# Sums of x made sooner, x copied back one chunk at a time, and one block of x kept at another address

## The chip, the cores and the metric

The kernel runs on one core of one Trainium2 chip. The metric is the device time of one execution in microseconds (us). Inside the core TensorE (PE) multiplies, VectorE (DVE) and ScalarE (ACT) work on tiles, GpSimd (POOL) and SyncE (SP) issue transfers among other things; each has an instruction queue of its own, which it works off in order, and waits on semaphores where it needs another's result.

## The reference

Two layers: a stick-breaking attention, then an RG-LRU block, each followed by a squared-ReLU MLP of width 4096, on 512 positions of width 1024. The change touches the two MLPs alone:

```python
def squared_relu_mlp(h, w1, w2):
    u = jax.nn.relu(h @ w1)
    return (u * u) @ w2
...
        h = rms_norm(x, norm_mlp[layer])
        x = x + squared_relu_mlp(h, mlp_w1[layer], mlp_w2[layer])
```

## The kernel before, in words

All matrices are f32, and each product is made of three f32r products: a number is split in a coarse part and a remainder, and coarse×coarse, coarse×remainder and remainder×coarse are added in PSUM. So every weight tile is first cast on ACT (`wh`) and subtracted on DVE (`wl`), and so is x.

**x.** x, scaled by the norm's gain, stands transposed in one tile `xg`: eight chunks of 128 features by 512 positions for the coarse part (`xgh`) and eight for the remainder (`xgl`), with margins of 64 elements (`FRONT`) at the ends and between the two. `Chunks` turns a chunk and columns into a place in the tile; its `down` holds two shifts in elements: the first for the first 256 columns of chunk 0, the second for all else. While the MLP's first quarter runs, both are 0. Then `x_down` sets them to 64 and 16 (`ASIDE`), and `lower` copies what is still needed of x down in the tile by as much. In the built program the 128-column blocks of the weights stand 512 bytes apart; after the shift by 64 elements the first columns of chunk 0 stand at a whole multiple of 512 bytes from them (this is the "distance 0"), everything else at 320 bytes past one.

**The MLP.** The 4096 hidden features are worked off in four quarters. The first quarter's up-projection (`squared`, eight output chunks c, plain products of 512 columns) is followed by its down-projection, and each later quarter is an "up" and a "down" of seven block products P1 to P7 with additions between blocks in the manner of Strassen (28 steps of a quarter: 14 of up, 14 of down). An up step is 24 matmuls of 256 columns, a down step 12 of 512. The products of up need sums of blocks of x: for each k of 0 to 3, `sums_of_x(k)` scales chunks k and 4+k on ACT and makes four sums of 256 columns on DVE, and `halves_of_sums(k)` splits them (casts on ACT, subtractions into `low` tiles on DVE). Chunk k must be through with `squared` before its sums may overwrite it in `xg`; sums made earlier are parked (`s3`, and the free eighth chunk of `bh` and `bl`), and `replace` copies them into `xg` later.

**What is made when, before.** In layer 0 the sums of k = 0 and 1 are made while the first up-projection's last output chunks c = 4 and 5 run, in layer 1 those of k = 0, 1 and 2 at c = 4, 5, 6. The others come while the first down runs: after its steps 5 and 6 (`place` 19 and 20) for k = 2 in layer 0 and k = 3 in layer 1, and after steps 10 and 11 (`place` 24 and 25) for k = 3 in layer 0. `replace` copies all parked sums at once after step 7 (`place` 21).

**What sets the order.** PE's order is the program's. On DVE and ACT, from the end of the first up-projection on, each instruction is chained to the one before it (`Ordered`), so they run as written; before that a scheduler merges the streams. `prepare` makes the weights of the step four ahead: a cast on ACT (`wh`), a subtraction on DVE (`wl`), and, where a product needs a sum of two weight blocks, an addition on DVE (`b<-b,b`) or, for P7 and P4, a transfer by POOL that adds the second block in memory to the first in place (L1089). In the first half of up the steps come in the order P1 P5 P6 P3 P7 P2 P4; P1, P6, P7 and P4 add up in one PSUM bank, whose state ACT copies out after P1, P6 and P7 (`u<-ps_acc`, in the second half `u<-ps_z`) before PE may go on in it.

Of the kernel before, what the change touches and what calls it, by code (L numbers as in the profile page):

```python
# [18 lines left out]
S = 512  # L19
D = 1024  # L20
C = D // P
# [6 lines left out]
ASIDE, FRONT = 16, 64  # L28
# [34 lines left out]
def hybrid_encoder(  # L63
# [40 lines left out]
    def f(ap):  # L104
        return ap.bitcast(F32)
# [28 lines left out]
    xgh, xgl = Chunks(0), Chunks(1)  # L134

    def x_down(*down):

        xgh.down = xgl.down = down
    bh = const.tile([P, C, S], F32R, tag="bh", name="bh")
    bl = const.tile([P, C, S], F32R, tag="bl", name="bl")  # L140

# [622 lines left out]
    HS = S // 2  # L764
# [21 lines left out]
    class Mlp:  # L786
# [157 lines left out]
        def halves_of_sums(self, k):  # L944
# [14 lines left out]
            self.A.copy(self.s41[:, k, :], v)  # L959
            self.V.tensor_tensor(low, v, f(self.s41[:, k, :]), ALU.subtract)  # L960

        LOWER = {15: (0, 0), 16: (1, 0), 17: (0, 1), 18: (0, 2), 22: (1, 1), 23: (1, 2)}

        def lower(self, i, part):

            def at(a, n):
                return x_t[:, a : a + n]

            def firsts(a):
                return at(a, 3 * S).rearrange("p (c s) -> p c s", s=S)[:, :, :HS]  # L970

            a = (xgh, xgl)[i].start
            if part:
                a += 2 * (part + 1) * S
                self.A.copy(at(a - ASIDE, 2 * S), at(a, 2 * S))
                return
            self.A.copy(at(a - FRONT, HS), at(a, HS))
            self.A.copy(firsts(a + S - ASIDE), firsts(a + S))

        def replace(self):  # L980

            for k in list(self.s3):
                self.A.copy(xgh[:, k, HS:], f(self.s3[k]))
                here = self.s2(k)
                del self.s3[k]
                self.A.copy(self.s2(k), f(here))

        def slots_of(self, p):

# [154 lines left out]
        def run(self, first, between, end):  # L1144
# [13 lines left out]
            def place(i):  # L1158

                return (i + self.STEPS // 2) % self.STEPS  # L1160
# [8 lines left out]
            def add(i, ahead=1):  # L1169

                if i >= len(steps) or i in done or steps[i][3] not in ("P5", "P6"):
                    return
                *what, name = steps[i]
                far = what[0] == "down" and (name, what[2]) in FARS
                if ahead > (5 if far else 2 if name == "P5" else what[0] == "up"):
                    return
                if steps.index((*what, {"P5": "P1", "P6": "P5"}[name])) in made:
                    done.add(i)

                    self.added(unit(i), name, far=far)  # L1180
# [11 lines left out]
            def prepare(i):  # L1192

                if i < len(steps) and steps[i][0] == "up" and steps[i][3] == "P7":
                    return
                if i - 1 in range(len(steps)) and i - 1 not in made and i > 2:
                    make(i - 1)
                if i < len(steps) and steps[i][0] == "down":
                    add(i, 0)
                    if waiting and place(i) in (20, 22, 23):  # L1200
                        self.split_slot(*waiting.pop(0))
                make(i)
                for n in range(i + 1, i + 6):
                    add(n, n - i)

            def last_sums(u, which):
                for to, a, b, how in which:
                    self.V.tensor_tensor(u[to], u[a], u[b], how)
# [23 lines left out]
            def leave(i):  # L1232

                ahead = i + 4
                if i < 0:
                    return
                kind, q4, p, name = steps[i]
                bank = sums[kind, q4, p if kind == "up" else 0][self.PRODUCTS[name][3]]
                if kind == "down":
                    if q4 == 0 and place(i) == 21:  # L1240
                        self.replace()
                    if p:
                        self.collect(name, 0, bank[0])
                    if steps[min(ahead, len(steps) - 1)][0] == "down":
                        add(ahead, 0)
                    if p:
                        self.collect(name, 1, bank[1])
                    prepare(ahead)
                    if later and place(i) > 15:
                        later.pop()()  # L1250
                    if q4 == 0:
                        x_down(FRONT, ASIDE)
                        if place(i) in self.LOWER:
                            self.lower(*self.LOWER[place(i)])

                        k = ({19: 2, 20: 2, 24: 3, 25: 3}, {19: 3, 20: 3})[self.layer].get(place(i))
                        if k:
                            (self.sums_of_x if place(i) in (19, 24) else self.halves_of_sums)(k)
                    return
                u, three = us[p], bank.rearrange("p (i n) -> p i n", i=2)  # L1260
                keep = {"P1": 0, "P6": 1, "P5": 2, "P7": 3}.get(name)
                if keep is not None:

                    self.A.copy(u[keep], three)
                at, x, y, op = {
                    "P3": (1, three, u[1], ALU.subtract),
                    "P7": (2, u[2], u[3], ALU.subtract),
                    "P2": (0, u[0], three, ALU.add),
                    "P4": (3, three, None, None),
                }.get(name, (None,) * 4)  # L1270
                if op:
                    self.V.tensor_tensor(u[at], x, y, op)
                if name == "P4":
                    def fourth(u=u, three=three, p=p):
                        self.A.activation(u[3], three, AF.Relu)
                        self.square(u[3])
                        if p:
                            last_sums(u, self.SUMS[:2])
                        else:
                            self.sums(p, slice(0, 2))  # L1280

                    if p:
                        fourth()
                    else:
                        later.append(fourth)
                elif later:
                    later.pop()()
                prepare(ahead)
                if op:
                    def rest(u=u, at=at):  # L1290
                        self.A.activation(u[at], u[at], AF.Relu)
                        self.square(u[at])
                        if p:
                            self.split_slot(p, u[at], at)

                    if p and name == "P3":
                        later.append(rest)
                    else:
                        rest()
                    if name == "P2" and not p:  # L1300
                        self.split(p, slice(0, 2), slice(0, 3), slice(0, 3))
                elif name == "P4" and p:
                    last_sums(u, self.SUMS[2:3])
                    self.split_slot(p, u[2], 5)
                    later.append(lambda: last_sums(u, self.SUMS[3:]))
                    waiting[:] = [(p, u[j], 3 + j) for j in (0, 1, 3)]
                elif name in ("P5", "P6") and p:
                    n = ("P5", "P6").index(name)
                    self.split(0, n, slice(0, 4), slice(3, 7))
# [36 lines left out]
        def quarters(self, between, end):  # L1346
            for c in range(C - 1):
                self.squared(c)
                p, i = c // 4, c % 4 // 2
                if c % 2:  # L1350
                    self.split(p, i, slice(0, 3), slice(0, 3))
                    self.sums(p, i)
                    self.split(p, i, slice(0, 4), slice(3, 7))
                if c == 0:
                    units = self.from_down(0)
                    self.load(units, *self.FROM_UP)
                if c < 2:

                    for n in range(4 * c, 4 * c + 4):
                        self.sq.chunk(n, x[n], e=V)  # L1360
                if c == C - 2:
                    self.rr = self.sq.inv_squares(self.bank())
                between(c)

                k = c - 4
                if k in range(2 + self.layer):
                    with tc.issue_after(self.squares.ins):
                        self.sums_of_x(k)
                        self.halves_of_sums(k)
            self.run(units, between, end)  # L1370
            self.blocks.close()
# [460 lines left out]
```

## Time and profile before

| | us |
|---|---|
| median of 3 runs | 1035.24 |
| lowest and highest | 1034.46, 1035.85 |
| the profiled execution | 1034.89 |
| its span on the core | 1033.2 |

PE's granted clock was 0.999 over the span. Layer 0's first down begins at 291.03 us and its first up at 329.93 us; layer 1's first down begins at 757.78 us and its first up at 796.80 us. In the rows of a timeline the first number is the start in us, the second the time of the group, then engine, line, operation and tiles; a bracket tells how long the engine had been idle before and on whom it waited. A matmul's own time overlaps with the next one's, so what a matmul costs is the distance from its start to the next start.

### The profile page before, as it was taken

Reading aid. Unit: us, or ns where it says so; the run is one execution under the profiler, and the core shown is the slowest. Engines: PE = TensorE matmul, PEld = TensorE weight load, DVE = VectorE, ACT = ScalarE, POOL = GpSimd, SP = SyncE. Lnnn points to the kernel's source line nnn. Section 1 sums busy time; section 2 is a strip of 40 time slices with the busy share of each in tenths; the row PEclk is TensorE's granted clock in tenths of the full one; section 3 lists DMA queues with packets and bytes.
Section 4 is the critical chain, followed back from the end, with each engine's and each line's share of the span. In section 5 each row is a group of like instructions: output and inputs, shape, how many; then the busy total and the mean of one; then the engine's idle time right before and its main releaser. Section 6 shows DMA issues by size and latency. Waiting matters only on the chain.

```text
span 1033.2 us, 15885 instructions
## 1 busy us (share of the span) xinstructions
PE 1022.3 (99%) x5868; PEld 892.2 (86%) x5868; DVE 862.9 (84%) x1152; ACT 713.5 (69%) x1104; POOL 174.6 (17%) x235
## 2 busy tenths in 40 slices
PE   9999999999999999999999999999999999999997
PEld 7888888888888988988988888888888988988986
DVE  6988787847789699799799889984689899798898
ACT  6777676836778674774765689964777774874866
POOL 0444444420010010010011210300000010010012
PEclk9999999999999999999999999999999999999999
DMA  7745454537546667677683464452436677677663
GB/s 233 220 121 143 107 154 103 153 108 279 143 82 183 167 154 196 164 158 191 162 233 83 132 179 122 119 202 83 102 80 185 164 163 189 165 159 195 165 125 105
DMA packets 52700, 159.41 MB, mean 154 GB/s; under 512 B 6672, under 2 KB 7952, under 8 KB 52624
## 3 DMA queue, kind: packets, MB, share of 16 engines
q1 hardware_dynamic: 41376, 119.35, 35.8%
q0 software_dynamic: 10528, 38.28, 22.3%
q8 instruction: 46, 0.75, 0.3%
q10 hardware_dynamic: 720, 0.79, 0.2%
q14 instruction: 30, 0.25, 0.1%
HBM read 137.41 MB, written 4.19 MB: 137 GB/s over the span
## 4 chain that ended last, share of the span: by engine, by line
PE 89%; DVE 4%; ACT 3%; issue 2%; DMA 1%; POOL 0%; SPq 0%; DVEq 0%; ACTq 0%; POOLq 0%
PE ps_t L1107 13%; PE ps_acc L1012 8%; PE ps_z L1012 7%; PE ps_acc L1107 7%; PE ps_acc L236 5%; PE ps_acc L238 5%; PE ps_acc L237 5%; PE ps_o L1012 4%; PE ps_z L1107 3%; PE ps_t L236 3%; PE ps_t L237 3%; PE ps_t L238 3%; PE ps_o L236 2%; PE ps_o L237 2%; PE ps_o L238 2%
## 5 line engine op out<-in xcount | busy, mean ns | idle before, releaser
L776 ACT CAST wh<-b 128x1024 fp32r<-128x1024 f32 x168 | 174.1, 1050 | 112.5 <-DVE b L776 73.9
L776 DVE TENSOR_TENSOR wl<-b,wh 128x1024 fp32r<-128x1024 f32 x168 | 204.2, 1221 | 45.4 <-ACT wh L776 44.7
L1089 POOL DMA_DIRECT2D b<-in_w_dn x40 | 35.0, 876 | 352.0 <-DVE b L776 265.6
L236 PE MATMUL ps_acc<-xg,wh 128*128 128x512 f32 x200 | 81.6, 408 | 0.0
L1012 PE MATMUL ps_z<-xg,wh 128*128 128x256 f32 x384 | 79.0, 277 | 0.8 <-ACT u L776 0.8
L238 PE MATMUL ps_acc<-xg,wh 128*128 128x512 f32 x200 | 78.3, 392 | 0.0
L237 PE MATMUL ps_acc<-xg,wl 128*128 128x512 f32 x200 | 78.3, 391 | 0.0
L231 DVE TENSOR_TENSOR wl<-raw,wh 128x512 fp32r<-128x512 f32 (+2 forms) x70 | 62.2, 914 | 15.0 <-ACT wh L229 14.8
L600 DVE TENSOR_TENSOR_SCAN scan<-keep,later 128x128 f32<-128x128 f32 (+1 forms) x64 | 59.5, 933 | 16.2 <-ACT keep L590 9.9
L776 ACT ACTIVATE u<-u 128x512 f32<-128x512 f32 x100 | 63.1, 632 | 9.5 <-DVE u L776 7.7
L229 ACT CAST wh<-raw 128x512 fp32r<-128x512 f32 (+2 forms) x70 | 50.6, 758 | 23.9 <-PE ps_acc L238 7.3
L1012 PE MATMUL ps_z<-xg,wl 128*128 128x256 f32 x240 | 66.4, 277 | 0.0
L1012 PEld LDWEIGHTS ps_z<-xg,wh 128*128 128x128 f32 x384 | 62.8, 188 | 1.2 <-ACT u L776 1.0
L1012 PE MATMUL ps_acc<-xg,wh 128*128 128x256 f32 x288 | 61.6, 278 | 1.2 <-ACT u L776 1.2
L1089 POOL DMA_DIRECT2D b<-in_w_up x24 | 20.9, 870 | 241.8 <-DVE b L776 90.5
L604 POOL TENSOR_TENSOR w<-w,scan 128x128 f32<-128x128 f32 (+1 forms) x64 | 51.4, 805 | 54.4 <-DVE scan L600 51.4
L776 DVE TENSOR_TENSOR b<-b,b 128x1024 f32<-128x1024 f32 x48 | 58.7, 1224 | 1.3
L776 DVE TENSOR_TENSOR u<-u 128x512 f32<-128x512 f32 (+1 forms) x92 | 54.9, 597 | 2.6 <-ACT u L776 1.1
L1012 PE MATMUL ps_acc<-low,wh 128*128 128x256 f32 x192 | 53.2, 277 | 0.1
L1012 PE MATMUL ps_acc<-xg,wl 128*128 128x256 f32 x192 | 53.2, 277 | 0.0
L776 ACT CAST wh<-raw 128x1024 fp32r<-128x1024 f32 x46 | 48.0, 1045 | 6.9 <-PE ps_acc L1107 6.9
L1107 PE MATMUL ps_t<-wh,bh 128*128 128x512 f32 x126 | 49.4, 392 | 0.4 <-DVE c L776 0.4
(383 smaller groups left out, 3277.1 us busy)
## 6 DMA issues: line engine op xcount, KB each, us to landing
b<-in_w_dn SPq DMA_DIRECT2D x48, 512.0 KB, 4.6
b<-in_w_dn POOLq DMA_DIRECT2D x40, 512.0 KB, 5.5
b<-in_w_up SPq DMA_DIRECT2D x36, 512.0 KB, 4.6
b<-in_w_up POOLq DMA_DIRECT2D x24, 512.0 KB, 5.5
raw<-in_w_m SPq DMA_DIRECT2D x16, 512.0 KB, 4.3
raw<-in_w_dn SPq DMA_DIRECT2D x16, 512.0 KB, 4.6
raw<-in_w_in SPq DMA_DIRECT2D x16, 512.0 KB, 4.6
raw<-in_w_qk SPq DMA_DIRECT2D x12, 512.0 KB, 3.7
```

The source lines that it names most:

```text
L229: A.copy(wh[:, k, :], raw[:, k, :])
L231: V.tensor_tensor(wl[:, k, :], raw[:, k, :], f(wh[:, k, :]), ALU.subtract)
L236: PE.matmul(ps, wh, ah, start=start, stop=False)
L237: PE.matmul(ps, wl, ah, start=False, stop=False)
L238: PE.matmul(ps, wh, al, start=False, stop=stop)
L600: V.tensor_tensor_scan(sc[:, S - n : S][:, ::-1], keep[:, :n][:, ::-1], later[:, S - n :][:, ::-1], 1.0, ALU.mult, ALU.max,)
L604: G.tensor_tensor(wt, wt, sc[:, S - n + 1 : S + 1], ALU.mult)
L776: ins = getattr(self.e, name)(*args, **kwargs)
L1012: PE.matmul(ps[:, i * HS : (i + 1) * HS], m, y, start=new and i == k == n == 0, stop=i == 1 and k == C // 2 - 1 and n == 2, skip_group_che ...
L1089: G.dma_start(out=unit[b].rearrange("p j n -> p (j n)"), in_=unit["src"](to), accum_op=ALU.add)
L1107: PE.matmul(ps, m, y[:, jj, cols], start=first and n == 0, stop=last and n == 2, skip_group_check=not new,)
```

## The change

Three things are edited. The sums of x move: in layer 0, k = 2 is made at c = 6 and k = 3 after steps 5 and 6, and nothing is left after steps 10 and 11; in layer 1, k = 0 and 1 are made at c = 4, k = 2 at c = 5, k = 3 at c = 6, and none during the down. `replace` copies one k per call, after steps 5, 7, 10 and 11. And of chunk 0's first columns only the remainder (`xgl`) is shifted by 64 elements; the coarse part is shifted by 16 like all else, so that it goes with the three chunks after it in one copy of four blocks instead of two copies.

```diff
     def x_down(*down):
-        xgh.down = xgl.down = down
+        xgh.down, xgl.down = (down[1],) * 2, down
...
+        REPLACE = 19, 21, 24, 25
         LOWER = {15: (0, 0), 16: (1, 0), 17: (0, 1), 18: (0, 2), 22: (1, 1), 23: (1, 2)}
...
-            def firsts(a):
-                return at(a, 3 * S).rearrange("p (c s) -> p c s", s=S)[:, :, :HS]
+            def firsts(a, n):
+                return at(a, n * S).rearrange("p (c s) -> p c s", s=S)[:, :, :HS]
...
-            self.A.copy(at(a - FRONT, HS), at(a, HS))
-            self.A.copy(firsts(a + S - ASIDE), firsts(a + S))
+            if i:
+                self.A.copy(at(a - FRONT, HS), at(a, HS))
+            a += S * i
+            self.A.copy(firsts(a - ASIDE, C // 2 - i), firsts(a, C // 2 - i))
...
         def replace(self):
-            for k in list(self.s3):
-                self.A.copy(xgh[:, k, HS:], f(self.s3[k]))
-                here = self.s2(k)
-                del self.s3[k]
-                self.A.copy(self.s2(k), f(here))
+            k = min(self.s3)
+            here = self.s2(k)
+            self.A.copy(xgh[:, k, HS:], f(self.s3.pop(k)))
+            self.A.copy(self.s2(k), f(here))
...
-                    if q4 == 0 and place(i) == 21:
+                    if q4 == 0 and self.s3 and place(i) in self.REPLACE:
                         self.replace()
...
-                        k = ({19: 2, 20: 2, 24: 3, 25: 3}, {19: 3, 20: 3})[self.layer].get(place(i))
-                        if k:
-                            (self.sums_of_x if place(i) in (19, 24) else self.halves_of_sums)(k)
+                        if self.layer == 0 and place(i) in (19, 20):
+                            (self.sums_of_x, self.halves_of_sums)[place(i) - 19](3)
...
-                k = c - 4
-                if k in range(2 + self.layer):
+                for k in ({4: (0,), 5: (1,), 6: (2,)}, {4: (0, 1), 5: (2,), 6: (3,)})[self.layer].get(c, ()):
                     with tc.issue_after(self.squares.ins):
                         self.sums_of_x(k)
                         self.halves_of_sums(k)
```

PE's order of matmuls, their shapes and operands stay; 48 of them (the coarse part's first columns of chunk 0, in the P1 of every up) read at another address. On POOL nothing moves, on SP one load of x back from memory moves three places up. On DVE and ACT the order changes at these places.

DVE in layer 0, from the last steps of the first down into the first up; `b` are weight blocks, `c` the output's sums, `x` the sums of x, `low` their remainders. Before:

```order
L776 TENSOR_TENSOR wl<-b_3728,wh 128x1024
L776 TENSOR_TENSOR b_3728<-b_3728,b_3730 128x1024
L776 TENSOR_TENSOR x<-x 128x256 x4
L776 SCALAR_TENSOR_TENSOR c_3131<-ps_z,rr,c_3131 128x512 x2
L776 TENSOR_TENSOR wl<-b_3728,wh 128x1024
L776 TENSOR_TENSOR b_3728<-b_3728,b_3732 128x1024
L776 TENSOR_TENSOR low<-x,xg 128x256 x2
L776 TENSOR_TENSOR low<-x,s_3138 128x512
L776 TENSOR_TENSOR wl<-b_3728,wh 128x1024
L776 TENSOR_TENSOR wl<-b_3732,wh 128x1024
```

and now, at the same place:

```order
L776 TENSOR_TENSOR wl<-b_3744,wh 128x1024
L776 TENSOR_TENSOR b_3744<-b_3744,b_3746 128x1024
L776 SCALAR_TENSOR_TENSOR c_3131<-ps_z,rr,c_3131 128x512 x2
L776 TENSOR_TENSOR wl<-b_3744,wh 128x1024
L776 TENSOR_TENSOR b_3744<-b_3744,b_3748 128x1024
L776 TENSOR_TENSOR wl<-b_3744,wh 128x1024
L776 TENSOR_TENSOR wl<-b_3748,wh 128x1024
```

The four sums and three remainders of k = 3 are gone from between the weights' instructions (P1's `wl`, the addition for P5, P5's `wl`, the addition for P6, P6's `wl`, P3's `wl`).

DVE in layer 1, at the end of the first up-projection, from the last `sl<-u,sh` of four blocks to the `wl` of the down's step 4. Before:

```order
L776 TENSOR_TENSOR low<-x,s_7742 128x256
L776 TENSOR_TENSOR x<-x 128x256
L776 TENSOR_TENSOR sl<-u,sh 128x1024
L776 TENSOR_TENSOR low<-x,bl 128x256
L776 TENSOR_TENSOR low<-x,s_7356 128x512
L776 TENSOR_TENSOR sl<-u,sh 128x768
L776 TENSOR_TENSOR wl<-b_7427,wh 128x1024
L776 TENSOR_TENSOR u<-u 128x256 x4
L776 TENSOR_TENSOR wl<-raw,wh 128x1024
L776 TENSOR_TENSOR b_7427<-b_7427,b_7429 128x1024
L776 TENSOR_TENSOR sl<-u,sh 128x1024
L776 TENSOR_TENSOR wl<-b_7427,wh 128x1024
```

and now:

```order
L776 TENSOR_TENSOR low<-x,s_7702 128x256
L776 TENSOR_TENSOR x<-x 128x256
L776 TENSOR_TENSOR low<-x,bl 128x256
L776 TENSOR_TENSOR sl<-u,sh 128x1024
L776 TENSOR_TENSOR sl<-u,sh 128x768
L776 TENSOR_TENSOR wl<-b_7429,wh 128x1024
L776 TENSOR_TENSOR u<-u 128x256
L776 TENSOR_TENSOR low<-x,s_7358 128x512
L776 TENSOR_TENSOR u<-u 128x256 x3
L776 TENSOR_TENSOR wl<-raw,wh 128x1024
L776 TENSOR_TENSOR b_7429<-b_7429,b_7431 128x1024
L776 TENSOR_TENSOR sl<-u,sh 128x1024
```

All seven instructions of one more k now stand ahead of, and one of them between, what the first down waits for. In layer 0 the same seven (of k = 2) stand at the same place, all ahead of the `sl<-u,sh 128x768`.

## The prediction

> **What bounds the kernel now.** First the page's head and its chain of waits:
>
> ```profile
> span 1033.2 us, 15885 instructions
> PE 1022.3 (99%) x5868; PEld 892.2 (86%) x5868; DVE 862.9 (84%) x1152; ACT 713.5 (69%) x1104; POOL 174.6 (17%) x235
> PE 89%; DVE 4%; ACT 3%; issue 2%; DMA 1%; POOL 0%; SPq 0%; DVEq 0%; ACTq 0%; POOLq 0%
> ```
>
> PE is busy for 1022.3 of 1033.2 us. The change leaves PE's list of matmuls alone, so it can only touch the stretches in which PE stands still or runs slower than its pace. The list of PE's waits names two that matter, both in an up step, on ACT:
>
> ```profile
> PE ps_acc L1012 <- ACT u L776: 1.2, 1, 1.2
> PE ps_z L1012 <- ACT u L776: 0.8, 1, 0.8
> ```
>
> A busy matmul hides a late start, so I read the starts themselves in PE's timeline of layer 0's first up:
>
> ```profile
> 333.84 0.28 PE L1012 MATMUL ps_acc<-s,wl 128*128 128x256 f32 x1
> 334.25 0.39 PE L1012 MATMUL ps_acc<-low,wh 128*128 128x256 f32 x1
> 334.47 0.28 PE L1012 MATMUL ps_acc<-s,wh 128*128 128x256 f32 x1
> ...
> 346.62 0.28 PE L1012 MATMUL ps_z<-xg,wh 128*128 128x256 f32 x1
> 348.06 0.38 PE L1012 MATMUL ps_acc<-xg,wh 128*128 128x256 f32 x1 [1.16 <-ACT u L776]
> 348.28 0.28 PE L1012 MATMUL ps_acc<-xg,wl 128*128 128x256 f32 x1
> ...
> 356.40 0.28 PE L1012 MATMUL ps_o<-low,wh 128*128 128x256 f32 x1
> 357.51 0.39 PE L1012 MATMUL ps_z<-xg,wh 128*128 128x256 f32 x1 [0.83 <-ACT u L776]
> 357.74 0.28 PE L1012 MATMUL ps_z<-xg,wl 128*128 128x256 f32 x1
> ```
>
> The pace is 0.11 from start to start. Against two such steps (0.22), the three places lose 0.63 - 0.22 = **0.4**, 1.66 - 0.22 = **1.4** and 1.34 - 0.22 = **1.1** us. No other up loses as much.
>
> **The change part by part.**
>
> *Sums of k = 3 leave the end of layer 0's first down.* The first place waits for the remainders (`low`) of k = 3 themselves; they are made long before now, so its 0.4 goes. The other two hang on this chain, in order of time:
>
> ```profile
> 327.23 1.79 DVE L776 TENSOR_TENSOR x<-x 128x256 f32<-128x256 f32 x4
> 328.94 1.40 DVE L776 SCALAR_TENSOR_TENSOR c<-ps_z,rr,c 128x512 f32<-128x512 f32 x2
> 330.26 1.22 DVE L776 TENSOR_TENSOR wl<-b,wh 128x1024 fp32r<-128x1024 f32 x1
> ...
> 332.65 0.75 DVE L776 TENSOR_TENSOR low<-x,xg 128x256 fp32r<-128x256 f32 x2
> 333.51 0.69 DVE L776 TENSOR_TENSOR low<-x,s 128x512 fp32r<-128x512 f32 x1
> 334.11 2.36 DVE L776 TENSOR_TENSOR wl<-b,wh 128x1024 fp32r<-128x1024 f32 x2
> ...
> 335.69 0.86 POOL L1089 DMA_DIRECT2D b<-in_w_up  x1 [6.93 <-DVE wl L776]
> ...
> 327.40 1.05 ACT L776 CAST wh<-b 128x1024 fp32r<-128x1024 f32 x1 [2.67 <-DVE b L776]
> 332.76 2.00 ACT L776 CAST wh<-b 128x1024 fp32r<-128x1024 f32 x2 [1.59 <-DVE b L776]
> 343.29 2.00 ACT L776 CAST wh<-b 128x1024 fp32r<-128x1024 f32 x2 [3.93 <-DMA b<-in_w_up]
> 347.44 0.57 ACT L776 COPY u<-ps_acc 128x512 f32<-128x512 f32 x1
> ...
> DMA to landing us min/median/max: 5.3/5.6/7.5
> ```
>
> DVE makes P6's `wl` at 334.11; that frees the block to which POOL's transfer at 335.69 adds the second one for P4; it lands after 7.5 us, the longest of its kind in this up (last row), at 343.2; ACT, in order, stands before P4's cast until then, and behind that cast stands its copy of the bank (347.44 to 348.01), for which PE waits at 346.62. So the wait's root is DVE, 16 us earlier. Without the sums, P5's `wl` needs only its cast, which ends at 327.40 + 1.05 = 328.45: 1.8 sooner than 330.26. The addition and the cast at 332.76 follow it, and without the three remainders (next start 334.11 - 332.65 = 1.46, of which the cast's round trip hides most) P6's `wl` starts at some 332.06: **2.05** sooner, and so does POOL's transfer. If it takes 7.5 us again, all of ACT after 343.29 comes 2.05 sooner: the copy ends at 345.96, PE arrives at 346.73 - 0.41 = 346.32, and the 1.4 are gone. At the second place PE then arrives 1.85 sooner and the copy comes 2.05 sooner, so of the 1.1 only some 0.3 go. If the transfer takes the median 5.6 us, all 1.1 go. SP's loads that run beside it are tied partly to this DVE chain and partly to PE, so I take a bit above the first end: **0.5** (0.3 to 1.1). The down's steps before 327 keep their DVE work (k = 3 has taken the place of k = 2), so nothing is gained there.
>
> *The same work lands on the start of the first downs.* It is four sums (1.79) and three remainders (0.75 + 0.69), 3.2 us on DVE, in each layer, and it stands ahead of the weights that the down's step 4 needs. What room there is:
>
> ```profile
> 287.00:293.40 6.40, 6.40 (x30) 5.29 (x29) 3.25 (x9) 3.20 (x6) 0.00 (x0) 1.00 0.00 0
> ...
> 743.60:760.30 16.70, 16.70 (x80) 13.92 (x79) 14.64 (x33) 14.20 (x26) 0.29 (x1) 1.00 0.32 64
> ...
> 760.29 0.96 DVE L776 TENSOR_TENSOR sl<-u,sh 128x768 fp32r<-128x768 f32 x1 [0.49 <-ACT sh L776]
> ...
> 767.62 2.36 DVE L776 TENSOR_TENSOR wl<-b,wh 128x1024 fp32r<-128x1024 f32 x2
> ...
> 768.66 0.39 PE L1107 MATMUL ps_acc<-wh,sh 128*128 128x512 f32 x1
> 768.90 0.50 PE L1107 MATMUL ps_acc<-wl,sh 128*128 128x512 f32 x1
> ```
>
> The columns after the length are PE, PEld, DVE, ACT. In layer 0 DVE has 6.40 - 3.25 = 3.15 us free before its `sl` at 293.4, just the 3.2; the room is cut in pieces and ACT gets its own part of k too (2.7 us, rows below), so I put **+0.3** (0 to 3.2). In layer 1 DVE is free for 16.70 - 14.64 = 2.06 of the stretch, and I count on 1.7 of it, since some is latency between dependent sums. From 760.29 to 767.62 it runs without a gap, and the `wl` that it begins then is taken by PE at 768.90 the moment that its first 1.22 are over: no slack. So **+1.5** there (1.1 to 3.2). What is queued behind is the whole chain of the down's weights, but each later step has a lead again once PE itself is late.
>
> *Sums leave layer 1's first down.* There PE loses time once, on DVE's collecting of the output:
>
> ```profile
> 790.62 0.39 PE L1107 MATMUL ps_z<-wh,sl 128*128 128x512 f32 x1
> 791.24 0.47 PE L1107 MATMUL ps_t<-wh,bh 128*128 128x512 f32 x1 [0.23 <-DVE c L776]
> ```
>
> At the down's pace of 0.23 this is 0.62 - 0.23 = 0.4. With 3.2 us less on DVE just before, it goes: **-0.4** (0 to -0.5).
>
> *One k per `replace`, and one copy for two in `lower`.* Two more casts per layer of 128x256 and one instruction less, all on ACT between steps 1 and 11 of the down, where DVE is the later one; ACT loses the scalings and casts of a whole k there. I count 0. Uncovered, the two casts are 0.7 us by the second of these rows, which with the other two are all of ACT's part of one k, 1.34 + 0.70 + 0.62 = 2.7 us:
>
> ```profile
> 323.38 1.34 ACT L776 ACTIVATE x<-x,colt 128x512 f32<-128x512 f32 x2
> ...
> 329.36 0.70 ACT L776 CAST xg<-x 128x256 fp32r<-128x256 f32 x2
> 329.96 0.62 ACT L776 CAST s<-x 128x512 fp32r<-128x512 f32 x1
> ```
>
> *The distance.* An up step is 24 matmuls. The starts of P1, P5 and P6 in an up without waits:
>
> ```profile
> 429.38 0.28 PE L1012 MATMUL ps_z<-xg,wh 128*128 128x256 f32 x1
> 432.14 0.28 PE L1012 MATMUL ps_o<-s,wh 128*128 128x256 f32 x1
> 434.86 0.28 PE L1012 MATMUL ps_z<-xg,wh 128*128 128x256 f32 x1
> ```
>
> P1, alone in reading the block at distance 0, takes 2.76; P5 takes 2.72. Twelve P1 (two layers, three ups, two halves) lose 12 x 0.04 = 0.5. Of the six matmuls of a P1 at that distance, four leave it: two thirds, **-0.3** (-0.5 if any one costs, 0 if it is the change of block that costs). The Trainium skill ("TensorE: Matmul & The Clock Gate", Step-by-step: what each phase is for) has weights and streamed operand come by two independent read ports, so that loading weights takes nothing from the running matmul; by that no address should matter, and this term would be 0. The trace's 2.76 against 2.72 leans against it.
>
> **Sum.** -0.4 - 1.4 - 0.5 + 0.3 + 1.5 - 0.4 + 0 - 0.3 = **-1.2** us against the profiled execution's 1034.89, which stands 0.35 under the median of the runs. So 1033.7 for an execution like the profiled one, and **1034.0** against the median of 1035.24.
>
> **Rivals.**
> - *The transfer is quick.* With the median 5.6 us it lands some 4 us sooner than now, and both waits of the up go whole: 0.6 more, and with DVE's room in layer 1 used fully 0.4 more again: -2.2, **1033.0**. For it: only this one transfer of its kind takes 7.5. Against: SP's loads that run beside it move up as well. The Trainium skill ("DMA: Bandwidth & Descriptors", Anatomy of one DMA — SWDGE (gpsimd) path) gives 2.0 us plus the bytes over 436 GB/s, an estimate of 3.2 us for 512 KB; by it the wait would be gone whole as well; the trace's least is 5.3.
> - *The transfer lands when it does now*, because the loads beside it, not its issue, set the end. Then PE only arrives 0.4 sooner and waits 0.4 longer; -0.4 - 1.4 - 0.5 turn to 0: +0.3 + 1.5 - 0.4 - 0.3 = +1.1, **1036.3**, slower. For it: 7.5 against 5.6 shows that something shares the engines.
> - *The backlog is not absorbed.* DVE's gaps at both starts end on ACT, and ACT gets 2.7 us of its own in them; if they stay, both starts cost the whole 3.2: 2.9 + 1.7 more than in the sum, +3.4, **1038.6**. It makes the kernel slower from 1.2 us above the sum's 1.8 on. Against: in the two stretches ACT is free for 3.20 and 2.50 us.
> - *The distance costs nothing*, P1 stays at 2.76: 1034.3.
>
> **How the numbers follow.** The forecast has 0.48, the quick transfer 0.20, the unmoved one 0.13, the backlog 0.11, the distance without effect 0.08. Faster by over 0.2% (about what a measurement of this kernel can tell from no change) means under 1033.2: half of the quick transfer's cases with some of the forecast's, 0.22. Slower means over 1037.3: the backlog and a few of the unmoved, 0.13. Within: 0.65. The forecast's own range is 1032.8 to 1035.3; to hold eight in ten I take 1031.9 to 1037.0.
>
> **What would show it.** Right: in layer 0's first up no start later than the pace at the places of P5 and P4, a wait of 0.3 to 0.8 before P6 of the second half; POOL's transfer for P4 issued two us sooner against PE; a new wait of 1 to 2 us within the first five steps of layer 1's first down, on `wl` by DVE, and less than 0.6 in layer 0's; P1 at 2.73 to 2.74. Wrong: P4's cast still ends its wait at the same time against PE; DVE idle in layer 1 before 760; or a wait where neither chain is.

## The result and the profile after

The changed kernel takes 1039.48 us in the median of 6 runs (1038.49 to 1040.19), the kernel before 1035.04 in 6 runs (1034.46 to 1035.94): a ratio of 1.0037, with a 95% interval of 1.0026 to 1.0048. It is slower; forecast were 1034.0 us, and the range ended at 1037.0. The head of the page of the changed kernel:

```profile
span 1037.8 us, 15891 instructions
PE 1027.9 (99%) x5868; PEld 900.6 (87%) x5868; DVE 862.2 (83%) x1152; ACT 715.7 (69%) x1106; POOL 168.8 (16%) x235
```

PE has the same 5868 matmuls and is busy for 5.6 us longer, at the same granted clock of 0.999. So the time did not come from waits alone, and I cut both traces at the first matmul of every up and down and compared the stretches:

| stretch (distance from start to start on PE) | before | after | difference |
|---|---|---|---|
| up to layer 0's first down | 289.90 | 290.52 | +0.6 |
| layer 0's first down | 38.90 | 39.11 | +0.2 |
| layer 0's first up | 41.72 | 39.57 | -2.2 |
| the other five ups, each | 38.17 | 39.57 | 5 x +1.40 |
| layer 1's first down | 39.03 | 40.16 | +1.1 |
| the later downs, together | | | -2.1 |
| layer 1's block between the two MLPs | 192.65 | 192.65 | 0 |
| behind the last matmul | 6.64 | 6.48 | -0.2 |

The first row has sums of x that were moved at its end, but its +0.6 is there at 216 us already, before any of them; from then on every matmul up to the down comes at the same distance as before. In the experiments below this stretch came out between 0.6 shorter and 0.1 longer than before, so that it scatters by that much. What decides is the fourth row. The timeline of the changed kernel at the P1, P5 and P6 whose starts the prediction quotes from 429.38 on:

```profile
428.19 0.28 PE L1014 MATMUL ps_z<-xg,wh 128*128 128x256 f32 x1
431.02 0.28 PE L1014 MATMUL ps_o<-s,wh 128*128 128x256 f32 x1
433.85 0.28 PE L1014 MATMUL ps_z<-xg,wh 128*128 128x256 f32 x1
```

P1 takes 2.83, where it took 2.76, and P5, none of whose addresses changed, takes 2.83 as well, where it took 2.72. That is 117.8 ns a matmul instead of 113.3, nowhere with a wait, and so in every up: 336 matmuls by 4.4 ns are 1.5 us, and with the 0.1 taken off that an up's two P1 cost over the pace before, they are the 1.4. The windows of one whole up, before and after (length, then PE's busy time and its instructions, with one or two that reach in from before, the granted clock, the transfers' share and their GB/s):

```profile
410.28:448.46 38.18, 38.18 (x338) 1.00 0.61 158
```

```profile
408.41:447.98 39.57, 39.57 (x337) 1.00 0.61 155
```

The transfers' share (0.61) is the same too. The rest went much as forecast. Layer 0's first up in the changed kernel, at the two places where PE waited for ACT before, with POOL's transfer and ACT's cast and copy:

```profile
347.60 0.28 PE L1014 MATMUL ps_z<-xg,wh 128*128 128x256 f32 x1
347.71 0.28 PE L1014 MATMUL ps_acc<-xg,wh 128*128 128x256 f32 x1
...
356.08 0.28 PE L1014 MATMUL ps_o<-low,wh 128*128 128x256 f32 x1
356.19 0.28 PE L1014 MATMUL ps_z<-xg,wh 128*128 128x256 f32 x1
...
334.52 0.86 POOL L1091 DMA_DIRECT2D b<-in_w_up  x1 [4.95 <-DVE wl L776]
...
340.88 1.05 ACT L776 CAST wh<-b 128x1024 fp32r<-128x1024 f32 x1 [0.86 <-DMA b<-in_w_up]
...
345.09 0.59 ACT L776 COPY u<-ps_acc 128x512 f32<-128x512 f32 x1
```

Both steps are 0.11, the pace: the waits are gone. POOL issues the transfer 334.52 - 330.75 = 3.77 us after the up's first matmul, where it was 335.69 - 329.93 = 5.76; it takes 6.3 us where it took 7.5, and the copy is through at 345.68, 1.9 us ahead of PE. And the start of layer 1's first down:

```profile
763.58 0.39 PE L1109 MATMUL ps_t<-wh,sh 128*128 128x512 f32 x1
764.17 0.50 PE L1109 MATMUL ps_t<-wl,sh 128*128 128x512 f32 x1 [0.20 <-DVE wl L776]
...
766.83 0.39 PE L1109 MATMUL ps_z<-wh,bh 128*128 128x512 f32 x1
767.49 0.50 PE L1109 MATMUL ps_z<-wl,bh 128*128 128x512 f32 x1 [0.27 <-DVE wl L776]
...
770.16 0.39 PE L1109 MATMUL ps_acc<-wh,sh 128*128 128x512 f32 x1
771.03 0.50 PE L1109 MATMUL ps_acc<-wl,sh 128*128 128x512 f32 x1 [0.48 <-DVE wl L776]
```

Three steps of 0.59, 0.66 and 0.87 stand where the pace is 0.23, each with one of 0.34 behind it: 1.77 us, all on `wl` by DVE.

### The profile page after: what moved, and what is told of

Read it like the earlier page. It is cut to its first block, busy times and chain, and to the rows that moved or that the text cites. A ratio compares the mean times of both kernels' runs of the same rounds, so it can differ in the third digit from the quotient of the medians.

```text
span 1037.8 us, 15891 instructions
## 1 busy us (share of the span) xinstructions
PE 1027.9 (99%) x5868; PEld 900.6 (87%) x5868; DVE 862.2 (83%) x1152; ACT 715.7 (69%) x1106; POOL 168.8 (16%) x235
## 4 chain that ended last, share of the span: by engine, by line
PE 90%; DVE 4%; ACT 2%; DMA 2%; issue 1%; ACTq 0%; POOL 0%; DVEq 0%; SPq 0%
PE ps_t L1109 15%; PE ps_acc L1014 10%; PE ps_z L1014 8%; PE ps_acc L1109 7%; PE ps_acc L236 5%; PE ps_o L1014 5%; PE ps_acc L238 5%; PE ps_acc L237 5%; PE ps_z L1109 3%; PE ps_t L237 2%; PE ps_t L236 2%; PE ps_t L238 2%; PE ps_o L236 2%; PE ps_o L237 2%; PE ps_o L238 2%; PE ps_t L622 1%
```

## The experiments

**Theory A.** An up has two paces, 113.3 and 117.8 ns a matmul, and keeps whichever it is in; a whole block at distance 0 (P1's k = 0) brings it to the faster, and what the change left of that block does not. **Theory B.** The slower pace comes from what the moved sums and copies do beside PE, or from entering the up without a wait.

**Undo the distance alone.** The changed kernel with both parts of chunk 0's first columns at distance 0 again:

```diff
-        xgh.down, xgl.down = (down[1],) * 2, down
+        xgh.down = xgl.down = down
...
-            if i:
-                self.A.copy(at(a - FRONT, HS), at(a, HS))
-            a += S * i
-            self.A.copy(firsts(a - ASIDE, C // 2 - i), firsts(a, C // 2 - i))
+            self.A.copy(at(a - FRONT, HS), at(a, HS))
+            self.A.copy(firsts(a + S - ASIDE), firsts(a + S))
```

> The changed kernel with the third edit undone: both parts of chunk 0's first columns are shifted by 64 elements again, the sums of x stay sooner and replace copies one k per call. Theory A (two paces: the matmuls of up run at 113.3 or at 117.8 ns from start to start, a block at distance 0 brings PE to the faster one, and one third of that block does not): twelve matmuls take 1.360 us nearly everywhere in up, PE's sum over up falls from 237.4 to some 229.0 us, and the time is 1039.5 - 8.4 = 1031 us. Theory B (the slower pace comes from the sums and copies that were moved, or from entering up without a wait): twelve matmuls still take 1.413 us and the time stays at 1039 to 1040 us.

Measured: 1033.53 us (10 runs), 0.9986 of before (0.9977 to 0.9996). Its timeline at the same P1, P5 and P6:

```profile
425.78 0.28 PE L1012 MATMUL ps_z<-xg,wh 128*128 128x256 f32 x1
428.54 0.28 PE L1012 MATMUL ps_o<-s,wh 128*128 128x256 f32 x1
431.26 0.28 PE L1012 MATMUL ps_z<-xg,wh 128*128 128x256 f32 x1
```

2.76 and 2.72, as before the change, with the moved sums and copies in place. Five ups take 38.17 us again; layer 0's first takes 38.64, 3.1 less than before; of the 0.47 that it has over 38.17 a short wait is 0.16, and the rest is a stretch at the slower pace behind that wait. Theory B falls. The time is 2.5 above Theory A's 1031: the six ups give 7.9 back of the 8.4 that it counted, and the later downs, 2.1 shorter than before in the changed kernel, are only 0.3 shorter here, which it had not counted.

**The distance alone.** The kernel before with the third edit and nothing else (the diff above, read backwards).

> The kernel before with the third edit alone (the coarse part of chunk 0's first columns shifted by 16 elements, the remainder by 64, one copy for two). Theory A: twelve matmuls of up take 1.413 us in all ups without waits; in layer 0's first up the waits take up a part of it; 5 ups of 28 half steps gain 28 x 0.053 = 1.5 us each less 0.1 for P1, so about 1035.0 + 7 = 1042 us. Theory B: 1.360 us outside P1 as before, 1035 us or a few tenths less.

Measured: 1040.08 us (4 runs), 1.0048 of before (1.0033 to 1.0063). P5 in it:

```profile
432.29 0.28 PE L1014 MATMUL ps_o<-s,wh 128*128 128x256 f32 x1
435.11 0.28 PE L1014 MATMUL ps_z<-xg,wh 128*128 128x256 f32 x1
```

2.82 with the old order of sums: the slower pace needs the third edit only. The five later ups take 39.57 each, and the later downs lose less than before, as in the changed kernel; so it is the slower up that brings this, not the moved sums (that the weights for the downs gain the time is likely, but not shown). Of 7.0 us that the pace takes in these ups, some 1.4 come back there, most of what the time stays under the 1042 expected.

Layer 0's first up is another matter here: it has its waits, and a wait can change the pace. It begins at the slower pace, with 2.83 for P1; behind a short wait (a step of 0.29 from 333.34) PE goes on at the faster one up to the long wait at 345.98, though none of these matmuls is at distance 0. Two starts 12 matmuls apart:

```profile
335.21 0.28 PE L1014 MATMUL ps_acc<-xg,wh 128*128 128x256 f32 x1
336.57 0.28 PE L1014 MATMUL ps_acc<-xg,wh 128*128 128x256 f32 x1
```

That is 1.36, 113.3 ns a matmul.

**The other part.** Here the coarse part stands at distance 0 and the remainder with all else at 320: four of P1's six matmuls stay, against two in the changed kernel.

```diff
-        xgh.down, xgl.down = (down[1],) * 2, down
+        xgh.down, xgl.down = down, (down[1],) * 2
...
-            if i:
+            if not i:
                 self.A.copy(at(a - FRONT, HS), at(a, HS))
+            i = 1 - i
             a += S * i
```

> The changed kernel with the two parts exchanged: the coarse part of chunk 0's first columns at distance 0, the remainder shifted by 16 elements. Theory A says nothing of how many of the three matmuls are needed: if two that follow each other are enough, twelve matmuls take 1.360 us after the first P1 and the time is about 1031 us; if all three are needed, 1.413 us and 1039.5 us. Theory B: 1.413 us, 1039.5 us.

Measured once: 1038.35 us. A single time says little; the pace is read from the trace. The starts of P1, P5 and P6:

```profile
427.48 0.28 PE L1015 MATMUL ps_z<-xg,wh 128*128 128x256 f32 x1
430.27 0.28 PE L1015 MATMUL ps_o<-s,wh 128*128 128x256 f32 x1
433.10 0.28 PE L1015 MATMUL ps_z<-xg,wh 128*128 128x256 f32 x1
```

P5 takes 2.83: twice as many matmuls at distance 0 don't help. But P1 takes 2.79, and its single steps tell more (below).

**No block at all.** Both parts of chunk 0's first columns shifted by 16 like the rest.

```diff
-        xgh.down, xgl.down = (down[1],) * 2, down
+        xgh.down = xgl.down = (down[1],) * 2 if down[1] else down
...
-            if i:
-                self.A.copy(at(a - FRONT, HS), at(a, HS))
-            a += S * i
-            self.A.copy(firsts(a - ASIDE, C // 2 - i), firsts(a, C // 2 - i))
+            self.A.copy(firsts(a - ASIDE, C // 2), firsts(a, C // 2))
```

> The changed kernel with nothing at distance 0: both parts shifted by 16 elements. Theory A: the slower pace throughout, 1.413 us for twelve, without the one step of 122 and 114 ns that P1 shows now, 1039.5 us within 0.7. Theory B: the same. A third theory, that the remainder alone at distance 0 does harm (brings PE to the slower pace, which it would not have by itself): 1.360 us and about 1031 us.

Measured once: 1038.61 us, with every half of every P (12 matmuls) at 1.41 us.

So the slower pace is what an up without waits enters with and keeps when nothing stands at distance 0, and the remainder left alone there does no harm of its own: it does nothing. The steps in ns of the first P1 of the up that begins at 410.28 us before, first half and second half (the first three of each are k = 0):

```
before           114 119 120 121 121 116 114 114 113 113 114 113 | 119 113 116 122 116 114 113 114 113 ...
after            118 117 122 114 118 118 117 118 118 118 117 119 | 117 118 121 114 119 117 118 117 119 ...
coarse alone     114 119 121 121 116 114 114 113 113 114 113 113 | 120 112 117 117 118 118 118 117 118 ...
none             117 118 118 118 117 119 117 118 118 117 118 118 | 118 117 119 117 118 118 117 118 118 ...
```

Before, the first half takes some 30 ns more than 12 x 113.3, and what comes out is 113.3 to the end of the up. With the coarse part alone the first half reaches 113 also, and the second half's block takes it back to 118. That asked for a run in which nothing is beside PE.

**Matmuls alone.** Nothing of the reference is computed; PE runs 3576 matmuls of an up's shape and weights' spacing.

```diff
+    for turn in range(3):
+        for s in SHIFTS:
+            ps = bank()
+            part(ps, s, 48)
+            A.copy(y[:, HS : 2 * HS], ps)
...
+            part(ps, HOME, 48, last=False)
+            part(ps, s, 3, new=False, last=False)
+            part(ps, HOME, 45, new=False)
```

> No part of the reference is computed: PE alone runs 3576 matmuls of 256 columns, f32r, in the order and with the weights' spacing of an up step, from one small set of weights and x that stays in place. First three times eight stretches of 48, one for each distance of weights from x past a multiple of 512 bytes (0, 64, ... 448), each after a pause of PE; then at distance 320 two times eight stretches of 48 + 3 + 45, the three in the middle at each of the eight distances, after a pause; then the same without pauses. Theory A (two paces at distance 320, a block at distance 0 sets the faster): 113 to 114 ns or 117 to 118 ns a matmul at 320, mostly 118 after a pause, 113 after the three at distance 0, and no change after three at 320. If the pace belongs to the distance and not to the history: one pace for each distance, the same before and after the three. If the paces come from what DVE, ACT and the transfers do beside PE: one pace everywhere, since nothing runs beside it here.

Measured: in its timeline two starts 24 matmuls apart, from the stretches at distance 0 and 320:

```profile
32.40 0.28 PE L46 MATMUL ps_z<-xg,wl 128*128 128x256 f32 x1
35.28 0.28 PE L46 MATMUL ps_z<-xg,wl 128*128 128x256 f32 x1
...
51.80 0.28 PE L46 MATMUL ps_z<-xg,wl 128*128 128x256 f32 x1
54.62 0.28 PE L46 MATMUL ps_z<-xg,wl 128*128 128x256 f32 x1
```

2.88 and 2.82 over 24. All eight distances, from the records (ns a matmul, the same in all three turns):

| distance past a multiple of 512 bytes | 0, 256 | 64, 320 | 128, 384 | 192, 448 |
|---|---|---|---|---|
| stretch of 48 after a pause | 120.0 | 117.8 | 118.5 | 117.8 |
| 320 in the second and third part, before and after the three | | 113.3 | | |

So the pace depends on the distance, in a pattern that repeats every 256 bytes, and at 64 past (our 320) on the history besides: 117.8 in the first part, 113.3 in the others. One expectation missed: after a pause the second part ran at 113.3 and not 118. Three matmuls at any other distance left the faster pace as it was, after at most five more steps of 118 to 123 ns. Since PE was never in the slower pace there, the run did not show that a block leads out of it. DVE, POOL and the transfers stand still beside these matmuls, and both paces are there; so they are PE's own.

**Matmuls alone, entered in the slower pace.** Of the same kind; the cases of a P1, pauses of several lengths, and stretches without a pause.

```diff
+            part(ps, 48, 32, 32, new=True, last=True)
+            pause(ps)
+            ps = bank()
+            part(ps, 48, new=True)
+            part(ps, 24, first=first)
+            part(ps, 72, last=True)
```

> No part of the reference is computed: as the kernel of matmuls alone before, with other stretches. (1) Two times six cases: 48 matmuls at distance 128, a pause, 48 at 320 (in the run before these went at 117.8 ns), then 24 like the two halves of a P1 whose k = 0 has another distance, then 72 at 320. The six: coarse and remainder both at 0; the remainder alone at 0; the coarse part alone at 0; none; both at 384; both at 448. Theory A (at 320 PE keeps one of two paces, and a whole block at distance 0 brings it to the faster): 113.3 ns in the last 72 where both are at 0; 117.8 with none and with the remainder alone, as in the changed kernel; the coarse part alone, which went to and fro in the whole kernel, may end at either. (2) At the faster pace a pause, eight times, after copies of 16 to 256 columns: if any pause sets the slower pace, 117.8 in all; if the pace outlasts a pause, 113.3 in all; if the moment of going on decides, some of each. (3) 48 at 0, 384, 448 and 320 with no pause around: 120.0, 118.5, 117.8 and 113.3 if the first run's paces belong to the distance, 113.3 in all if they came from the pause. If the slow pace of the changed kernel came from something beside PE (DVE, ACT, transfers), (1) shows 113.3 in all six.

Measured: only the first of the twelve cases entered at 117.8, the other eleven at 113.3, against expectation. That first one is the case in question, both parts at 0. Its starts 12 matmuls apart, two ahead of the block and two behind it:

```profile
41.22 0.28 PE L49 MATMUL ps_z<-xg,wl 128*128 128x256 f32 x1
42.64 0.28 PE L49 MATMUL ps_z<-xg,wl 128*128 128x256 f32 x1
...
46.82 0.28 PE L49 MATMUL ps_z<-xg,wl 128*128 128x256 f32 x1
48.18 0.28 PE L49 MATMUL ps_z<-xg,wl 128*128 128x256 f32 x1
```

1.42 ahead, 1.36 behind, to the end of the stretch; and its steps are, to the nanosecond, those of the kernel before. It is the only case of its kind among the matmuls alone; in the whole kernels with the block in place it is there in every up. In the second turn, entered at the faster pace, it stays there.

In these two runs x moves and the weights stay, so x's own address, and not its distance from the weights, could be what counts. The built programs decide that: the block at distance 0 begins 32 bytes past a multiple of 256 in the kernel before and 128 past one here, the weights likewise, and the steps are the same.

The coarse part alone, entered at the faster pace: 12 matmuls ahead, and six inside the first half.

```profile
88.62 0.28 PE L49 MATMUL ps_z<-xg,wl 128*128 128x256 f32 x1
89.98 0.28 PE L49 MATMUL ps_z<-xg,wl 128*128 128x256 f32 x1
...
91.69 0.28 PE L49 MATMUL ps_z<-xg,wl 128*128 128x256 f32 x1
92.40 0.28 PE L49 MATMUL ps_z<-xg,wl 128*128 128x256 f32 x1
```

1.36 over 12, then 0.71 over 6 (118); behind the second half the steps are at 113 again (second line below): the coarse part alone switches the pace each time that it comes. From the faster, two halves lead back to the faster; in the whole kernel, from the slower, two halves lead back to the slower. In steps:

```
both at 0, from the slower     114 119 120 121 121 116 114 114 113 113 114 113 | 119 113 116 122 116 114 113 114 113 ...
coarse alone, from the faster  119 113 116 118 117 119 117 118 118 118 117 118 | 114 119 121 121 116 114 114 113 113 ...
```

The remainder alone, here entered at the faster pace, leaves it as it was (119 119 124 118, then 113); that it doesn't lead out of the slower one is shown by the whole kernels only (the changed one and the one with the distance alone). Of eight pauses at the faster pace, four went on at 113.3 and four at 117.8. One of each kind, with 12 matmuls between the second and the third row:

```profile
321.94 0.38 PE L49 MATMUL ps_z<-xg,wh 128*128 128x256 f32 x1 [0.52 <-ACT y L57]
323.52 0.28 PE L49 MATMUL ps_z<-xg,wl 128*128 128x256 f32 x1
324.88 0.28 PE L49 MATMUL ps_z<-xg,wl 128*128 128x256 f32 x1
...
355.19 0.38 PE L49 MATMUL ps_z<-xg,wh 128*128 128x256 f32 x1 [0.38 <-ACT y L57]
356.82 0.28 PE L49 MATMUL ps_z<-xg,wl 128*128 128x256 f32 x1
358.24 0.28 PE L49 MATMUL ps_z<-xg,wl 128*128 128x256 f32 x1
```

By the step over the pause, from start to start: 607, 660, 713 and 767 ns with the slower pace behind it, 592, 633, 686 and 792 with the faster. So neither shorter nor longer pauses belong to one pace, and a few ns make the difference: among the twelve cases above, the one that entered at 117.8 has a step of 797 over its pause, the other eleven 795 or 796. It seems to be the moment of going on that decides; by what rule, these runs don't show. Without pauses the distances 0, 384, 448 and 320 gave 120.0, 118.7, 117.8 and 113.3, and each time 320 went back to 113.3.

**A version that keeps both gains.** Both parts at distance 0, layer 0's sums in the new order, layer 1's made where the kernel before makes them.

```diff
-                        if self.layer == 0 and place(i) in (19, 20):
+                        if place(i) in (19, 20):
...
-                for k in ({4: (0,), 5: (1,), 6: (2,)}, {4: (0, 1), 5: (2,), 6: (3,)})[self.layer].get(c, ()):
+                for k in ({4: (0,), 5: (1,), 6: (2,)}, {4: (0,), 5: (1,), 6: (2,)})[self.layer].get(c, ()):
```

> As the run with both parts at distance 0, and layer 1's sums of x are made when the kernel before makes them (k = 0, 1, 2 at c = 4, 5, 6, k = 3 after steps 5 and 6 of the first down); layer 0 keeps the new order. Theory A (the ups' pace hangs on the block at distance 0 alone; of the moved sums layer 0's bring 3.2 us and cost 0.2, layer 1's cost 1.7 and bring 0.5): the waits at the start of layer 1's first down go (-1.7), the one before its step with the collected output comes back (+0.5), so 1.2 us under the run with both parts at distance 0 (1033.5): 1032.3, 0.9975 of before. If the waits at layer 1's start were there for another reason than its sums: 1033.5 again.

Measured: 1032.53 us (7 runs, 1031.90 to 1033.25), 0.9973 of before (0.9962 to 0.9984): faster than both kernels. The three waits at layer 1's start are gone, but of the 1.2 us against the first experiment the traces show less: layer 1's first down takes 39.67 where that one takes 40.13. Most of what is missing goes to `replace`. It copies one k already after step 5 now, and its two copies stand on ACT ahead of a cast for which DVE waits before it makes the sums of k = 3 and collects the output:

```profile
774.05 0.41 ACT L776 CAST xg<-s 128x256 fp32r<-128x256 f32 x1
774.36 0.41 ACT L776 CAST xg<-bh 128x256 fp32r<-128x256 f32 x1
774.67 1.05 ACT L776 CAST wh<-b 128x1024 fp32r<-128x1024 f32 x1
...
775.75 1.23 DVE L776 TENSOR_TENSOR wl<-b,wh 128x1024 fp32r<-128x1024 f32 x1 [0.73 <-ACT wh L776]
...
776.99 1.80 DVE L776 TENSOR_TENSOR x<-x 128x256 f32<-128x256 f32 x4
...
778.71 1.40 DVE L776 SCALAR_TENSOR_TENSOR c<-ps_t,rr,c 128x512 f32<-128x512 f32 x2
778.72 0.39 PE L1107 MATMUL ps_acc<-wh,sl 128*128 128x512 f32 x1
...
779.60 0.47 PE L1107 MATMUL ps_t<-wh,bh 128*128 128x512 f32 x1 [0.49 <-DVE c L776]
```

The cast starts 774.67 - 754.14 = 20.53 us after the down's first matmul, where before the change it started 777.68 - 757.78 = 19.90 after it, and the sums and the collecting come 0.64 later as well. PE reaches its place as before (24.58 after that matmul, 24.52 before) and loses a step of 0.88 there, where before the step was 0.30 and the pace is 0.23. A version that leaves these two copies behind the cast was not run. The intervals of this run and the first experiment overlap, so that it beats the first experiment is read from the traces, not from the times.

## Why the prediction was wrong

**The distance: the step that failed.** The prediction put it at -0.3, as two thirds of the 0.04 us by which a P1 is longer than a P5, "alone in reading the block at distance 0", with 0 and -0.5 as its ends. The 0.04 was read rightly: it is the toll of passing the block. But P5 was taken as the pace without the block, and it is the pace that the block had just set. Without it P5 takes 2.83, and the term is 7.0 us in five ups and 1.0 in layer 0's first (39.57 - 38.17 = 1.4, of which 0.4 were there before), less 1.7 that come back in the later downs (2.1 shorter in the changed kernel, 0.3 in the first experiment): 6.2, where the two medians are 5.95 apart. The third edit alone makes the kernel before 1.0048 times as long; with it undone, the same change makes it 0.9986.

The trace of before had it in view. Behind the wait that ends at 348.06 PE goes on at the slower pace until the next P1. With the prediction's row at 348.28, 12 matmuls ahead of the first of these:

```profile
349.69 0.28 PE L1012 MATMUL ps_acc<-xg,wl 128*128 128x256 f32 x1
...
353.80 0.28 PE L1012 MATMUL ps_o<-s,wh 128*128 128x256 f32 x1
355.16 0.28 PE L1012 MATMUL ps_o<-s,wh 128*128 128x256 f32 x1
```

1.41 for 12 matmuls of P4, none of them at distance 0; then P1 with its block from 350.99 on; then 1.36 for 12 of P5. Two paces of one instruction in one trace were the sign, and the prediction called the pace "0.11 from start to start" and did not ask.

**The rule on two read ports.** The Trainium skill ("TensorE: Matmul & The Clock Gate", Step-by-step: what each phase is for) gives weights and streamed operand a port each, so that loading takes nothing from the matmul. With nothing else beside PE the distance alone moved the pace from 113.3 to 120.0 ns, so for these f32r matmuls of 256 columns with new weights each the measurement decides against what the prediction drew from that rule, that no address matters. Whether the two reads meet at a port or elsewhere, no run shows.

**Layer 0's first up (-0.4 - 1.4 - 0.5).** Right in its mechanism: the transfer is issued 1.99 us sooner against PE, the "two us" of the text, and it lands sooner by more. All waits are gone, 3.2 us instead of 2.3: the 0.6 of the second place that the sum kept as a wait before P6, and 0.2 at 363 that it had left out. That is the rival of the quick transfer: 6.3 us against 7.5. In the changed kernel the slower PE helps; in the first experiment, at the old pace, some 0.15 of the waits remain.

**The starts of the first downs (+0.3, +1.5).** Layer 0's down is 0.2 longer. In layer 1 the three waits are 1.8, less 0.1 that stood at 768.66 before: 1.7, inside its bounds, on `wl` by DVE, and in the steps named.

**Layer 1's first down (-0.4).** The steps at 790.62, 782.30 and around lost 0.7 over the pace before and lose 0.1 now: -0.6, a little past the term's end of -0.5. Together with the start, +1.1.

**`replace` and `lower` (0).** No wait in the changed kernel ends on one of their copies. In the last version, in which layer 1 makes sums during the down again, the earlier copies cost the 0.6 shown above, so the 0 holds for the change as it was made and not for `replace` by itself.

Without the distance the sum was -0.9, and the run that leaves it out measured 1033.53 against 1034.79, -1.3. That they come so near is in part luck: in that run's trace, its fastest execution, the stretches behind the first add up to -2.2, since the up's waits gave more than was forecast and the later downs 0.3 that no term had. Five of six terms stood in their mechanism; one of the smallest was the one that decided. The rival of the backlog, 1038.6, came near the time by chance: DVE's new work cost what the forecast said.

## What to carry to other kernels

Before an edit of an address is priced by its own few matmuls, look at whether the same instruction has more than one pace in the trace, and what stands where it turns from one to the other: a cheap thing may be what holds the state of everything behind it. A matmul's cost is read from start to start, over a stretch long enough to tell 113 from 118 ns; the time of one matmul (0.28 at either) and the list of waits show neither. And of a change that is made of several, measure the parts: here two edits were worth -1.3 us and the third +5 to +6.

## What the runs showed of the hardware

For f32r matmuls of 128x256 with new weights each, at a granted clock of 0.995 or more, the distance of the weights' block from the streamed operand in the partition sets the pace, repeating every 256 bytes: 120.0 ns at 0, 118.5 at 128, 117.8 at 192, and at 64 either 113.3 or 117.8. At 64 past PE keeps the pace that it has, the slower over the 336 matmuls of a whole up, the faster over the 144 between two P1; a pause can go on at either, and a few matmuls at another distance can bring it over. Which of the reads meet, and why three of k = 0 at distance 0 lead to the faster pace from both sides while the two of the coarse part switch it and the one of the remainder does nothing, no run here shows.
